# A SwiGLU down projection in sliding ranges of K, with shorter runs for its stored operands, in a hybrid transformer block

## The chip, the cores and the metric

One core of one Trainium2 chip. The metric is the device time of one execution in microseconds (us); of a kernel the median of its runs counts. Engines are named as in the profile: PE (TensorE) with PEld for its weight loads, DVE (VectorE), ACT (ScalarE), POOL (GpSimd) and SP (SyncE); here POOL and SP mostly issue DMAs, POOL on queue q0 and SP on queue q1.

## The reference

One layer of a diffusion backbone over 512 latent tokens (and 256 context tokens), width 2048. A modulation row `silu(c) @ w_mod + b_mod` gives six rows of 2048: shift, scale and gate for the mixer and for the feed-forward part. A recurrent and a windowed attention mixer feed one output projection; then comes the part that the change is about:

```python
x = x + gt_m * (concat([hg_lat, at_lat]) @ w_out)
h = modulate(rms_norm(x, norm_ffn_g), sh_f, sc_f)
gate, up = split(h @ w_gate_up)                 # 2048 -> 2 x 5632
x = x + gt_f * ((silu(gate) * up) @ w_down)     # 5632 -> 2048
```

All arrays are float32.

## The kernel before

Every product of float32 operands is made of three matmuls (`mm3`): each operand is split into a high part, rounded on ACT, and a low part, the difference formed on DVE; high x high, high x low and low x high are summed in PSUM.

The feed-forward part works on 2 x 2 blocks with a scheme of seven products (`PRODUCTS`, line 1369). So an operand is not four blocks but seven split sums of them, and a **step** (`run_step`, line 1570) is 7 products x 2 halves x 3 = 42 matmuls of 128 x 256 into seven half-used pairs of PSUM regions (`banks`). For each step SP loads two pieces of weights, 256 KB each (`st_load`, line 1393, tile `fx`, three buffers); DVE forms three sums (`st_sums`), ACT the high part `fh` (`st_high`), DVE the low part `fl` (`st_low`), each two steps ahead of the matmuls.

*Up stage*: 22 groups of 256 columns (`N_UP`), each of 8 steps over K = 2048; 176 steps. The eight operand sets of this stage are formed from x1 (`turn`, `form`). After a group's last step `evac_up` (line 1484) combines the seven results on DVE, applies the SiLU, forms the seven sums of the result, splits them (`hl`, two tiles of 128 x 1792, 896 KB each) and stores them into the DRAM buffer `sf_d` with POOL's queue: a set for the down stage.

*Down stage*: 22 such sets are the K of the product, 88 steps. Only eight sets fit into SBUF (`new_set`, line 1456, tiles `a`). K is cut into four ranges, `SPANS = (6, 6, 5, 5)` sets, and for each range the four blocks of 512 output columns (two runs of 256 in either half of the width) are visited in turn: 16 **visits** of 6 or 5 steps. At a visit's end `evac_down` (line 1539) combines the seven results with seven DVE operations into `c`, and POOL stores c in four DMAs of 256 KB to `y_d`, plainly in the first range and with an accumulating DMA in the next two. In the last range `prepare_down` (line 1519) has loaded y_d, x1 (`x1_d`, stored by POOL in `add_gated`, line 1306) and the gate row; y_d x gate + x1 is formed ahead, and c x gate is added to it and stored to the output by SP.

A set is used for the last time in a range's fourth visit. After its last step (`last_use`, line 1612) the next set takes its place, by two loads of 896 KB on POOL's queue, in runs of 7 KB. The first eight sets take the places of the up stage's during its last group.

The order of instructions on each engine is that of the code, with one exception: side work (here the modulation rows, `mod_gate` and `mod_cols`, in `mod_lane`) is woven in by a planner (`Estimate`, `Lane`), which keeps a clock for each engine and steps such a task when its operands should be there and DVE and ACT are not ahead of PE. `mod_gate` sums a row's 512 columns over K with 16 DVE operations from eight loads of 512 KB (`m_w`, SP), reduces over partitions with one matmul and stores the row in DRAM (`gtf_d`, the feed-forward gate). All tasks stand in `mod_tasks` (line 687 on) and are added before the recurrence. Since every operation passes through one wrapper, the profile gives line 130 for all; tiles tell them apart.

## Time and profile before

| what | value |
|---|---|
| median of 3 runs | 2716.01 us (2715.44 to 2721.18) |
| the profiled execution | 2721.39 us |
| its span | 2719.6 us |
| mean granted clock of PE, share of full speed | 0.97 |
| bytes moved by DMA | 488.81 MB, 180 GB/s on average |
| reloads of the sets (a from sf_d) | 44 x 896 KB, 9.8 us from issue to landing |
| loads of w_down | 176 x 256 KB, 3.7 us |
| loads of w_gate_up | 352 x 256 KB, 3.3 us |

The span lies within the profiled execution, which lasts 1.8 us longer. The up stage's matmuls run from 1239 to 2188 us, the down stage's from there to 2710 us. The granted clock has two levels, 1.2 and 2.4 GHz; 1.00 in a window means the upper one throughout. A busy time of PE counts a matmul at the lower level as long as it took there.

### The profile page before, as it was taken

To read this page: it belongs to the slowest core of one execution; us is meant where nothing else is said; L and a number is where in the kernel's file an instruction comes from. 1 tells how busy PE (TensorE), PEld (TensorE's weight loads), DVE (VectorE), ACT (ScalarE), POOL (GpSimd) and SP (SyncE) were. 2 spreads that over 40 slices of the span, in tenths; PEclk is the share of its full clock that TensorE was granted. 3 is DMA by queue.
4 is the path that set the end of the run, shared out by engine and by line. 5 is a ranking of instruction groups with operands and counts; after the bars stand their busy time and mean duration, and the time that the engine had idled before them with its cause. 6 is when DMAs were issued, how large, how long until landed. Compare 5 with 4: busy or idle time off the path is not lost.

```text
span 2719.6 us, 44137 instructions
## 1 busy us (share of the span) xinstructions
PE 2557.2 (94%) x17119; PEld 2317.3 (85%) x17119; DVE 2119.3 (78%) x3706; ACT 1060.6 (39%) x1529; POOL 219.9 (8%) x429
## 2 busy tenths in 40 slices
PE   7999999999999999997999999999999799898987
PEld 4579887878777877776999999999999789898986
DVE  4478967787899977566788888888889586766798
ACT  4244444447333332344444443434344233332322
POOL 0000010000111211100000000000000101121221
PEclk9999999999999999998999999999999899998998
DMA  9978677762654335541444444444444655677773
GB/s 347 303 262 262 214 234 224 228 193 59 203 178 126 105 120 184 174 153 55 124 156 145 147 159 144 144 163 155 136 162 153 251 202 210 197 202 197 190 205 121
DMA packets 328739, 488.81 MB, mean 180 GB/s; under 512 B 20305, under 2 KB 233458, under 8 KB 327762
## 3 DMA queue, kind: packets, MB, share of 16 engines
q1 hardware_dynamic: 284320, 354.50, 41.2%
q0 software_dynamic: 30832, 118.85, 13.5%
q10 hardware_dynamic: 13378, 12.65, 1.4%
q8 instruction: 134, 2.20, 0.3%
q14 instruction: 75, 0.61, 0.1%
HBM read 414.08 MB, written 71.84 MB: 179 GB/s over the span
## 4 chain that ended last, share of the span: by engine, by line
PE 32%; DMA 9%; DVE 8%; issue 2%; SPq 1%; ACT 0%; DVEq 0%; ACTq 0%
PE mm L130 16%; PE aux L130 16%; DMA fx<-in_w_down_dram 7%; DVE fl L130 4%; DVE big L130 3%; DVE fx L130 2%; DMA fx<-in_w_gate_up_dram 1%; SPq L130 1%; DMA gtr<-gtf_d 0%; ACT fh L130 0%; DVEq L130 0%; ACTq L130 0%
## 5 line engine op out<-in xcount | busy, mean ns | idle before, releaser
L130 ACT ACTIVATE fh<-fx 128x1792 fp32r<-128x1792 f32 x264 | 448.0, 1701 | 739.4 <-DVE fx L130 291.5
L130 DVE TENSOR_TENSOR fl<-fx,fh 128x1792 fp32r<-128x1792 f32 x264 | 532.6, 2019 | 60.6 <-ACT fh L130 58.9
L130 DVE TENSOR_TENSOR fx<-fx 128x256 f32<-128x256 f32 (+1 forms) x816 | 409.5, 510 | 213.3 <-DMA fx<-in_w_down_dram 105.9
L130 PE MATMUL mm<-a,fh 128*128 128x256 f32 x2464 | 478.6, 285 | 13.5 <-ACT a L130 12.1
L130 PE MATMUL aux<-a,fh 128*128 128x256 f32 x2464 | 475.4, 284 | 1.0 <-ACT fh L130 1.0
L130 PEld LDWEIGHTS mm<-a,fh 128*128 128x128 f32 x2464 | 388.9, 192 | 15.2 <-ACT a L130 13.0
L130 PEld LDWEIGHTS aux<-a,fh 128*128 128x128 f32 x2464 | 387.8, 191 | 1.3 <-ACT fh L130 1.2
L130 PE MATMUL aux<-a,fl 128*128 128x256 f32 x1232 | 351.6, 285 | 18.8 <-DVE fl L130 18.8
L130 PE MATMUL mm<-a,fl 128*128 128x256 f32 x1232 | 351.1, 285 | 0.0
L130 ACT ACTIVATE wh<-wr 128x512 fp32r<-128x512 f32 x376 | 227.3, 627 | 313.1 <-PE mm L130 175.9
L130 DVE TENSOR_TENSOR wl<-wr,wh 128x512 fp32r<-128x512 f32 x376 | 251.1, 685 | 89.0 <-ACT wh L130 88.3
L130 PE MATMUL mm<-wh,hT 128*128 128x512 f32 x896 | 298.6, 402 | 4.0 <-ACT hT L130 3.0
L130 PE MATMUL mm<-fh,a 128*128 128x256 f32 x1232 | 276.1, 290 | 16.5 <-DVE big L130 13.3
L130 PE MATMUL aux<-fh,a 128*128 128x256 f32 x1232 | 276.1, 290 | 7.0 <-DVE big L130 3.7
L130 PE MATMUL mm<-hT,wh 128*128 128x512 f32 x768 | 251.6, 404 | 0.0
L130 PEld LDWEIGHTS aux<-a,fl 128*128 128x128 f32 x1232 | 233.7, 190 | 19.7 <-DVE fl L130 19.7
L130 PEld LDWEIGHTS mm<-fh,a 128*128 128x128 f32 x1232 | 218.3, 198 | 19.5 <-DVE big L130 14.9
L130 PEld LDWEIGHTS mm<-a,fl 128*128 128x128 f32 x1232 | 234.1, 190 | 0.0
L130 PEld LDWEIGHTS aux<-fh,a 128*128 128x128 f32 x1232 | 217.7, 197 | 10.2 <-DVE big L130 5.2
L130 DVE SCALAR_TENSOR_TENSOR m_acc<-m_w,c_col,m_acc 128x512 f32<-128x512 f32 x240 | 178.8, 745 | 51.8 <-DMA m_w<-in_w_mod_dram 50.1
L130 PEld LDWEIGHTS mm<-wh,hT 128*128 128x128 f32 x896 | 169.4, 189 | 55.7 <-issue 8.6
L130 PE MATMUL aux<-fl,a 128*128 128x256 f32 x616 | 178.8, 290 | 23.3 <-DVE fl L130 23.3
(273 smaller groups left out, 4068.0 us busy)
## 6 DMA issues: line engine op xcount, KB each, us to landing
fx<-in_w_gate_up_dram SPq DMA_DIRECT2D x352, 256.0 KB, 3.3
wr<-in_w_in_dram SPq DMA_DIRECT2D x144, 512.0 KB, 4.6
m_w<-in_w_mod_dram SPq DMA_DIRECT2D x128, 512.0 KB, 4.7
fx<-in_w_down_dram SPq DMA_DIRECT2D x176, 256.0 KB, 3.7
sf_d<-big POOLq DMA_DIRECT2D x44, 896.0 KB, 4.1
a<-sf_d POOLq DMA_DIRECT2D x44, 896.0 KB, 9.8
ring<-in_w_mod_dram SPq DMA_DIRECT2D x64, 512.0 KB, 8.8
wr<-in_w_out_dram SPq DMA_DIRECT2D x36, 512.0 KB, 4.4
```

The lines of the kernel that those rows point to most:

```text
L130: return f(*a, **k)
```

## The change

- **Ranges that slide.** `ENDS` names for each of the 16 visits the set at which it stops; a visit starts where the visit of the same columns four earlier stopped. The visits have 2, 3, 5, 6, 6, 6, 6, 6, 6, 6, 6, 6, 8, 7, 5 and 4 steps (88 as before), and sets come free one or two to a visit, from the fourth visit on.
- **Columns.** A visit covers 512 columns that lie side by side, so a row of a w_down piece is one run of 2 KB, not two of 1 KB.
- **Stored sums.** `sf_d` is laid out so that stores and reloads have runs of 1 KB, 896 in a DMA, not 128 of 7 KB.
- **Gate and residual.** x1 is stored into `y_d` as the base. Each of the first 12 visits multiplies c by the gate (one DVE operation of 128 x 2048, a step later) and accumulates it into y_d with one DMA of 1 MB; the last four load y_d with one DMA and add. The gate's 512 columns are loaded at each visit.
- **Weight loads.** From step 8 on a step issues the load for four steps on, not three.
- **Gate row.** The four tasks for `gtf_d` join `mod_lane` at the start of the out-projection.

```diff
@@ -32,7 +32,7 @@
 RING = 5
 SC = 256
 N_UP = D_FF // SC
-SPANS = (6, 6, 5, 5)
+ENDS = (2, 3, 5, 6, 8, 9, 11, 12, 14, 15, 17, 18, 22, 22, 22, 22)
 RSQRT_SEED = float(0x5F3759DF)
 
 
@@ -194,9 +194,8 @@
     s_d = dram.tile([16, P, P], F32, name="s_d")
     gtm_d = dram.tile([1, D], F32, name="gtm_d")
     gtf_d = dram.tile([1, D], F32, name="gtf_d")
-    x1_d = dram.tile([T, D], F32, name="x1_d")
     y_d = dram.tile([T, D], F32, name="y_d")
-    sf_d = dram.tile([2 * N_UP, P, 7 * SC], F32R, name="sf_d")
+    sf_d = dram.tile([2 * N_UP, 7, P, SC], F32R, name="sf_d")
 
 
     ident = const.tile([P, P], F32, name="ident")
@@ -686,7 +685,6 @@
 
     mod_tasks = [mod_gate(j, 2 * D, gtm_d) for j in range(4)]
     mod_tasks += [mod_cols(mp, j, w) for j in range(4) for w in range(2)]
-    mod_tasks += [mod_gate(j, 5 * D, gtf_d) for j in range(4)]
 
 
 
@@ -1303,7 +1301,7 @@
             if squares:
                 act.activation(tm, x1[j][:, t, :], AF.Square, accum_out=ssj[:, t, j:j + 1])
                 if t == NT - 1:
-                    pool.dma_start(x1_d[:, 512 * j:512 * j + 512].rearrange("(t p) d -> p t d", p=P), x1[j])
+                    pool.dma_start(y_d[:, 512 * j:512 * j + 512].rearrange("(t p) d -> p t d", p=P), x1[j])
         return evac
 
     def mix_pools(st, right):
@@ -1331,6 +1329,8 @@
                 n[0] += 1
         return upto
 
+    for j in range(4):
+        mod_lane.add(mod_gate(j, 5 * D, gtf_d))
     m_st = ExitStack()
     gp = m_st.enter_context(tc.tile_pool(name="gp", bufs=1))
     mT = mix_pools(m_st, 0)
@@ -1379,16 +1379,14 @@
             u.src = [w_gate_up[(s + 8 * h) * P:(s + 8 * h + 1) * P, :].rearrange("p (u n) -> p u n", u=2)
                      [:, :, SC * g:SC * g + SC] for h in range(2)]
             steps.append(u)
-    n0 = 0
-    for b, n in enumerate(SPANS):
-        for j in range(4):
-            for s in range(n0, n0 + n):
-                u = Step()
-                u.up, u.g, u.b, u.a, u.first, u.last = False, j, b, 8 + s, s == n0, s == n0 + n - 1
-                u.src = [w_down[(2 * s + h) * P:(2 * s + h + 1) * P, :].rearrange("p (u n) -> p u n", u=2)
-                         [:, :, SC * j:SC * j + SC] for h in range(2)]
-                steps.append(u)
-        n0 += n
+    for v, e in enumerate(ENDS):
+        n0 = ENDS[v - 4] if v >= 4 else 0
+        for s in range(n0, e):
+            u = Step()
+            u.up, u.g, u.b, u.a, u.first, u.last = False, v % 4, v // 4, 8 + s, s == n0, s == e - 1
+            u.src = [w_down[(2 * s + h) * P:(2 * s + h + 1) * P, 2 * SC * (v % 4):2 * SC * (v % 4) + 2 * SC]
+                     .rearrange("p (u n) -> p u n", u=2) for h in range(2)]
+            steps.append(u)
 
     def st_load(i):
         if i < len(steps):
@@ -1507,64 +1505,51 @@
         yield
         dve.tensor_tensor(hl[1], xx[:, 1:8, :], hl[0].bitcast(F32), op=ALU.subtract)
         for i in range(2):
-            pool.dma_start(sf_d[2 * g + i].bitcast(F32), hl[i].bitcast(F32).rearrange("p f n -> p (f n)"))
-        yield
-
-    def rows_of(d, h, n, j):
-        c0 = 1024 * n + SC * j
-        return d[2 * P * h:2 * P * h + 2 * P, c0:c0 + SC].rearrange("(t p) n -> p t n", p=P)
-
-    QUADS = ((0, 1), (0, 0), (1, 1), (1, 0))
-
-    def prepare_down(j):
-
-        z = est.tile(xg, [P, 4, 512], F32, "big", "big", 4)
-        x1t = est.tile(xg, [P, 4, 512], F32, "big", "big", 4)
-        gt = est.tile(fx, [P, 2, SC], F32, "gtr", "gtr", 1)
-        for n in range(2):
-            pool.dma_start(gt[:, n, :], gtf_d[0:1, 1024 * n + SC * j:1024 * n + SC * j + SC].to_broadcast([P, SC]))
-        for k, (h, n) in enumerate(QUADS):
-            pool.dma_start(hf(z[:, k, :]), rows_of(y_d, h, n, j))
-            pool.dma_start(hf(x1t[:, k, :]), rows_of(x1_d, h, n, j))
-        yield
-        for k, (h, n) in enumerate(QUADS):
-            dve.tensor_tensor(hf(z[:, k, :]), hf(z[:, k, :]), gt[:, n:n + 1, :].to_broadcast([P, 2, SC]), op=ALU.mult)
-        yield
-        dve.tensor_tensor(z, z, x1t, op=ALU.add)
-        prepared[j] = z, gt
-        yield
+            pool.dma_start(sf_d[2 * g + i].bitcast(F32).rearrange("f p n -> p f n"), hl[i].bitcast(F32))
+        yield
+
+    def rows_of(d, j):
+        return d[:, 2 * SC * j:2 * SC * j + 2 * SC].rearrange("(a p) n -> p a n", p=P)
+
+    def quad(c, h, n):
+
+        return c[:, 2 * h:2 * h + 2, SC * n:SC * n + SC]
+
+    def prepare_down(j, fin):
+
+        gt = est.tile(fx, [P, 512], F32, "gtr", "gtr", 1)
+        pool.dma_start(gt, gtf_d[0:1, 512 * j:512 * j + 512].to_broadcast([P, 512]))
+        z = None
+        if fin:
+            z = est.tile(xg, [P, 4, 512], F32, "big", "big", 4)
+            pool.dma_start(z, rows_of(y_d, j))
+        prepared[j] = gt, z
 
     prepared = {}
 
     def evac_down(j, b, banks):
-        p1, p2, p6, p7, q4, q5, p3 = banks
-        fin = b == len(SPANS) - 1
+        p1, p2, p6, p7, q4, q5, p3 = (hf(x) for x in banks)
         c = est.tile(xg, [P, 4, 512], F32, "big", "big", 4)
-        r, t = c[:, 1, :], c[:, 3, :]
-
-        def done(k):
-            h, n = QUADS[k]
-            ck = hf(c[:, k, :])
-            if fin:
-                z, gt = prepared[j]
-                dve.tensor_tensor(ck, ck, gt[:, n:n + 1, :].to_broadcast([P, 2, SC]), op=ALU.mult)
-                dve.tensor_tensor(c[:, k, :], c[:, k, :], z[:, k, :], op=ALU.add)
-                sp_q.dma_start(rows_of(out, h, n, j), ck)
-            elif b == 0:
-                pool.dma_start(rows_of(y_d, h, n, j), ck)
-            else:
-                pool.dma_start(rows_of(y_d, h, n, j), ck, accum_op=ALU.add)
-
+        c11, r, c21, t = (quad(c, h, n) for h, n in ((0, 1), (0, 0), (1, 1), (1, 0)))
         act.activation(r, p1, AF.Copy)
-        dve.tensor_tensor(c[:, 0, :], p2, r, op=ALU.add)
+        dve.tensor_tensor(c11, p2, r, op=ALU.add)
         dve.tensor_tensor(r, p6, r, op=ALU.add)
         dve.tensor_tensor(t, r, p7, op=ALU.subtract)
-        dve.tensor_tensor(c[:, 2, :], t, q4, op=ALU.add)
+        dve.tensor_tensor(c21, t, q4, op=ALU.add)
         dve.tensor_tensor(r, q5, r, op=ALU.subtract)
         dve.tensor_tensor(t, q5, t, op=ALU.subtract)
         dve.tensor_tensor(r, p3, r, op=ALU.add)
-        for k in (0, 2, 3, 1):
-            done(k)
+        gt, z = prepared[j]
+        if z is None:
+            yield
+            dve.tensor_tensor(c, c, gt[:, None, :].to_broadcast([P, 4, 512]), op=ALU.mult)
+            pool.dma_start(rows_of(y_d, j), c, accum_op=ALU.add)
+        else:
+            for h, n in ((0, 1), (1, 1), (1, 0), (0, 0)):
+                ck = quad(c, h, n)
+                dve.tensor_tensor(ck, ck, gt[:, None, SC * n:SC * n + SC].to_broadcast([P, 2, SC]), op=ALU.mult)
+                dve.tensor_tensor(ck, ck, quad(z, h, n), op=ALU.add)
+                sp_q.dma_start(quad(rows_of(out, j), h, n), ck)
         yield
 
     def run_step(i, hooks):
@@ -1587,11 +1572,14 @@
     turn(0, 0)
     turn(0, 1)
     form(0)
-    pending = list(range(8, 8 + sum(SPANS)))
+    pending = list(range(8, 8 + N_UP))
     last_use = {u.a: i for i, u in enumerate(steps)}
     tail = []
     for i, u in enumerate(steps):
-        st_load(i + 3)
+        if i <= 8:
+            st_load(i + 3)
+        if i >= 8:
+            st_load(i + 4)
         st_sums(i + 2)
         st_high(i + 2)
         hooks = {}
@@ -1600,11 +1588,11 @@
         run_step(i, hooks)
         form(i + 1)
         st_low(i + 2)
-        if not u.up and u.b == len(SPANS) - 1 and u.first:
-            tail.append(prepare_down(u.g))
         for g in list(tail):
             if next(g, tail) is tail:
                 tail.remove(g)
+        if not u.up and u.first:
+            prepare_down(u.g, u.b == len(ENDS) // 4 - 1)
         if u.last:
             g = evac_up(u.g, u.banks) if u.up else evac_down(u.g, u.b, u.banks)
             next(g)
@@ -1613,7 +1601,7 @@
             n = pending.pop(0)
             new_set(n)
             for k in range(2):
-                pool.dma_start(sets[n][k].bitcast(F32).rearrange("p f n -> p (f n)"), sf_d[2 * (n - 8) + k].bitcast(F32))
+                pool.dma_start(sets[n][k].bitcast(F32), sf_d[2 * (n - 8) + k].bitcast(F32).rearrange("f p n -> p f n"))
 
 
 _INS = ["x", "c", "ctx", "c_ctx", "w_mod", "b_mod", "norm_mix_g", "norm_ffn_g", "w_in", "hg_lb",
```

What this does to the order on the queues is seen at two places. On POOL, the kernel before at the end of the down stage's first range (a: sets, reloaded from sf_d):

```order
L130 DMA y_d<-big 128x2x256 x12
L130 DMA a_22726<-sf_d 128x1792
L130 DMA a_22727<-sf_d 128x1792
L130 DMA a_22782<-sf_d 128x1792
L130 DMA a_22783<-sf_d 128x1792
L130 DMA a_22838<-sf_d 128x1792
L130 DMA a_22839<-sf_d 128x1792
L130 DMA a_22894<-sf_d 128x1792
L130 DMA a_22895<-sf_d 128x1792
L130 DMA a_22950<-sf_d 128x1792
L130 DMA a_22951<-sf_d 128x1792
L130 DMA y_d<-big 128x2x256 x4
```

and the changed kernel from the start of its down stage:

```order
L130 DMA y_d<-big 128x4x512
L130 DMA gtr<-gtf_d 128x512
L130 DMA y_d<-big 128x4x512
L130 DMA gtr<-gtf_d 128x512
L130 DMA a_22314<-sf_d 128x7x256
L130 DMA a_22315<-sf_d 128x7x256
L130 DMA y_d<-big 128x4x512
L130 DMA gtr<-gtf_d 128x512
L130 DMA a_22370<-sf_d 128x7x256
L130 DMA a_22371<-sf_d 128x7x256
L130 DMA a_22654<-sf_d 128x7x256
L130 DMA a_22655<-sf_d 128x7x256
```

Twelve y_d stores and then five sets in a row have become one accumulation, the gate's load and one or two sets a visit.

On SP, in the out-projection (wr: weights of that projection; io: its other operand; gt_c: the mixer's gate; fx: first weights of the up stage), the kernel before:

```order
L130 DMA gt_c<-gtm_d 128x512
L130 DMA wr<-in_w_out_dram 128x2x512 x6
L130 DMA io<-mix_d 128x512 x3
L130 DMA wr<-in_w_out_dram 128x2x512
L130 DMA io<-mix_d 128x512 x3
L130 DMA wr<-in_w_out_dram 128x2x512
L130 DMA io<-mix_d 128x512 x2
L130 DMA wr<-in_w_out_dram 128x2x512
L130 DMA fx<-in_w_gate_up_dram 128x2x256 x3
L130 DMA wr<-in_w_out_dram 128x2x512
L130 DMA fx<-in_w_gate_up_dram 128x2x256 x3
L130 DMA wr<-in_w_out_dram 128x2x512 x3
```

and the changed kernel:

```order
L130 DMA gt_c<-gtm_d 128x512
L130 DMA wr<-in_w_out_dram 128x2x512 x3
L130 DMA m_w<-in_w_mod_dram 128x2x512 x3
L130 DMA wr<-in_w_out_dram 128x2x512
L130 DMA m_w<-in_w_mod_dram 128x2x512
L130 DMA wr<-in_w_out_dram 128x2x512
L130 DMA m_w<-in_w_mod_dram 128x2x512 x2
L130 DMA wr<-in_w_out_dram 128x2x512
L130 DMA m_w<-in_w_mod_dram 128x2x512 x2
L130 DMA wr<-in_w_out_dram 128x2x512 x3
L130 DMA fx<-in_w_gate_up_dram 128x2x256
L130 DMA io<-mix_d 128x512 x2
```

Loads of w_mod for the feed-forward gate (m_w), 22 in all, now stand between the weights; before, all of them came earlier. Among the weights of the feed-forward part SP's order is the same in both kernels, but for one or two loads that change places with output stores at the end.

## Rows read from the trace of the kernel before

**Rows 1.** The page's head: the span, and busy time (share) xinstructions by engine.

```profile
span 2719.6 us, 44137 instructions
PE 2557.2 (94%) x17119; PEld 2317.3 (85%) x17119; DVE 2119.3 (78%) x3706; ACT 1060.6 (39%) x1529; POOL 219.9 (8%) x429
```

**Rows 2.** Windows: stretch, length, busy (x) by engine, PEclk, DMA share, GB/s.

```profile
1400.00:1800.00 400.00, 400.00 (x3334) 399.91 (x3333) 353.35 (x446) 166.93 (x119) 10.68 (x20) 1.00 0.46 151
2100.00:2719.60 619.60, 540.51 (x4227) 530.87 (x4225) 454.98 (x584) 182.61 (x123) 102.22 (x134) 0.93 0.64 198
2200.00:2300.00 100.00, 99.27 (x828) 98.36 (x828) 80.94 (x103) 35.32 (x23) 11.84 (x18) 1.00 0.51 172
```

**Rows 3.** Timeline at the end: start us, us, engine, line, operation.

```profile
2710.09 0.28 PE L130 MATMUL aux<-fh,a 128*128 128x256 f32 x1
...
2710.71 1.28 DVE L130 TENSOR_TENSOR big<-mm,big 128x512 f32<-128x512 f32 x2
2711.91 0.68 DVE L130 TENSOR_TENSOR big<-aux,big 128x512 f32<-128x512 f32 x1
```

**Rows 4.** The chain that ended last, down stage: start us, us, what.

```profile
2158.12 20.03 DMA fx<-in_w_down_dram
...
2429.95 21.00 DMA fx<-in_w_down_dram
```

**Rows 5.** Waits from 2120 to 2720 us: total us, times, longest us.

```profile
DVE fx L130 <- DMA fx<-in_w_down_dram: 105.9, 32, 11.2
...
PE aux L130 <- DVE fl L130: 42.1, 10, 9.6
...
DVE fx L130 <- DMA fx<-in_w_gate_up_dram: 25.3, 3, 12.8
...
PE mm L130 <- DVE big L130: 13.3, 11, 3.0
...
PE aux L130 <- DVE big L130: 3.7, 7, 2.1
```

**Rows 6.** DMA queues from 2162 to 2176 us: packets, MB, share of 16 engines.

```profile
q0 software_dynamic: 771, 4.90, 84.9%
q1 hardware_dynamic: 823, 0.79, 17.2%
```

**Rows 7.** DMA queues from 2256 to 2263 us, where one visit's y_d is stored.

```profile
q0 software_dynamic: 320, 1.05, 41.3%
```

**Rows 8.** DMA queues from 1188 to 1200 us, SP loading in 2 KB runs.

```profile
q1 hardware_dynamic: 701, 1.37, 36.3%
```

**Rows 9.** DVE by shape, 2120 to 2720 us: busy us, mean ns | idle.

```profile
L130 DVE TENSOR_TENSOR fl<-fx,fh 128x1792 fp32r<-128x1792 f32 x95 | 191.2, 2018 | 14.7 <-ACT fh L130 14.6
L130 DVE TENSOR_TENSOR fx<-fx 128x256 f32<-128x256 f32 x186 | 77.6, 421 | 3.7
L130 DVE TENSOR_TENSOR fx<-fx 128x512 f32<-128x512 f32 x93 | 63.6, 687 | 131.2 <-DMA fx<-in_w_down_dram 105.9 <-DMA fx<-in_w_gate_up_dram 25.3
...
L130 DVE TENSOR_TENSOR big<-big 128x2048 f32<-128x2048 f32 x4 | 9.1, 2282 | 0.0
```

**Rows 10.** Timeline at a gate row's matmul; in brackets the idle time before it.

```profile
720.64 2.04 PE L130 MATMUL aux<-m_acc,ones 128*128 128x512 f32 x2 [6.27 <-DVE hP L130]
```

**Rows 11.** Windows behind that matmul and in the out-projection, columns as in rows 2.

```profile
720.00:740.00 20.00, 19.36 (x73) 15.13 (x74) 17.64 (x58) 6.66 (x10) 2.54 (x8) 0.87 0.67 200
1000.00:1200.00 200.00, 192.55 (x883) 157.35 (x882) 122.69 (x210) 69.86 (x141) 15.88 (x38) 0.99 0.55 178
```

**Rows 12.** Waits of the whole span, the sums of the modulation rows.

```profile
DVE m_acc L130 <- DMA m_w<-in_w_mod_dram: 50.1, 45, 3.0
```

**Rows 13.** POOL's groups, columns as in rows 9.

```profile
L130 POOL DMA_DIRECT2D y_d<-big x48 | 50.9, 1158 | 271.7 <-DVE big L130 271.4 <-issue 0.3
```

**Rows 14.** DMA queues from 2530 to 2540 us, accumulating into y_d.

```profile
q0 software_dynamic: 797, 0.77, 57.4%
```

## The prediction, made before the changed kernel ran

> **What bounds the kernel now.** I read the page first: TensorE (PE) is busy 94% of the 2719.6 us [rows 1], so time can only go where PE idles or runs at the lower clock. The windows then show where that is. In the middle of the up stage 3334 matmuls fill 400.00 us at clock 1.00: 0.120 us for one, so 42 x 0.12 = 5.04 us for a step. From 2100 us to the end 4227 matmuls run at a mean clock of 0.93 [rows 2]. At 0.120 us they would need 507 us. The last matmul starts at 2710.09 and takes 0.28 [rows 3], which leaves 9.2 us of evacuation and stores behind it. So 619.6 - 507 - 9.2 = **103 us** are lost in the down stage and the last two up groups: 70 as idle time (619.6 - 540.5 busy - 9.2) and 33 as matmuls at the lower of the two clock levels (540.5 - 507), which follow the idle times. The stage is not slow as such: from 2200 to 2300 us PE is busy 99.27 of 100 [rows 2].
>
> The chain that ended last says what ends the idle time: single weight loads of 256 KB with pieces of 20 and 21 us [rows 4]. The waits agree: VectorE (DVE), which makes the sums of the weights, waits 105.9 us for w_down and 25.3 for w_gate_up, and PE behind it 42.1 us for the low parts [rows 5]. The DMA view of such a stretch says why. For 14 us queue 0 (POOL: reloads of the sets) and queue 1 (SP: weights) share the 16 engines, whose shares sum to 102%: 771 packets with 4.90 MB against 823 with 0.79 MB [rows 6]. They take turns about one for one, but a packet of POOL holds 6.4 KB on average and takes 0.849 x 16 x 14 / 771 = 0.247 us (7 KB: 0.28), one of SP 1 KB and 0.047 us. So the weights get 0.79 MB / 14 us = 56 GB/s, and a step needs 512 KB in 5.04 us = 104 GB/s. Ten or so such loads of 896 KB stand in one burst behind the last quarter of a range.
>
> **The change, part by part.**
>
> *Ranges that slide.* The bytes stay: 14 of the 22 sets are reloaded during the down stage, each 1.84 MB. But one or two sets come free in a visit instead of up to six in every fourth. The first of these loads is issued ten steps into the stage, and no set is used before 16 steps (81 us) have passed after its load: two sets take 3.7 MB / 300 GB/s = 12 us. Their place behind a visit's accumulation on POOL's queue, which waits for a multiplication one step later, costs 5 us of these 81, so nothing.
>
> *Runs of 1 KB for the sets, 2 KB for w_down.* What a turn takes now comes from two rows. In the stores of y_d, also runs of 1 KB, 1.05 MB took 0.413 x 16 x 7 = 46 us of engine time, 0.044 us for each KB, in 320 packets, few enough for four runs or 4 KB in one (1.05 MB is 256 times 4 KB) [rows 7]: 0.18 us. A 2 KB run of SP took 0.363 x 16 x 12 / 701 = 0.10 us [rows 8]. A pair of turns is 0.28 us, and the weights get 16 x 2 KB / 0.28 us = 115 GB/s, above the 104 they need. So I take the whole **-103**. Bounds: -103 (nothing is left to win) and -52, where half has a cause that I don't see.
>
> *The first burst stays.* While the last up group runs, eight sets and two stores, 18 MB, are moved, and w_gate_up keeps its 1 KB runs: 16 x 1 KB / (0.05 + 0.18) = 71 GB/s for some three steps of loads. Two steps of weights lie ready. Between 0 and the 25.3 us of now [rows 5], nearer to the low end: **+4**.
>
> *Short visits first.* A visit's end costs DVE seven operations of 0.68 [rows 3] and now a multiplication of 2.28 [rows 9]: 7.1 us. A step costs 0.687 + 2 x 0.421 + 2.018 = 3.55 [rows 9]. Visits 0 to 3 have 16 steps: 16 x 3.55 + 4 x 7.1 + 9.7 for the last up group (the same seven, two products, sums, low part) = 95 us of DVE against 80.6 of PE. Operations overlap by 0.08 us (0.68 long, 0.60 apart [rows 3]), 109 of them by 9: 86. Up to 5.6 us behind, or 0 if DVE starts ahead: **+4**. The whole stage fits: 88 x 3.55 + 16 x 4.8 + 12 x 2.28 + 32 x 0.68 + 9.7 = 447, with the overlap of 521 operations 405, against 443.5 for PE.
>
> *Ends of visits.* PE waits 13.3 + 3.7 = 17.0 us for banks that DVE still reads [rows 5]. There are 16 visits as before, and some of these waits only stand behind late weights. Between 0 and 17: **+8.5**.
>
> *Gate row later.* Its sums leave the recurrence, where PE waited 6.27 us before the row's matmul [rows 10] and ran the next 20 us at 0.87 (2.6 us) [rows 11]: up to -8.9. Three gates' sums, 48 operations of 0.75 us, and 22 loads of 512 KB enter the out-projection. There DVE has 122.7 of 200 us [rows 11], so 36 more fit, and 178 GB/s become 236, a share of 0.73 for 0.55. The loads stand on SP between those of w_out; late, they hold up DVE by up to 3.0 us each, 1.1 on average [rows 12], which its slack covers. The last gate's matmul and store now stand just ahead of the sum of squares at the stage's end: between 0 and those 8.9, taken at 2.5. Sum **-6.4**.
>
> *The rest is nothing.* One accumulation of 1 MB for four of 256 KB, x1 as the base in y_d: 4 MB less to read, and DVE's 12 x 2.28 in place of 16 x 0.68 + 4 x 2.28, covered as above. POOL issues a store of 256 runs in 1158 ns [rows 13]; 896 runs at four times that, 88 times, are 408 us of an engine that is 8% busy [rows 1], with 16 steps of cover; with that cover gone a set would come 4 us later. The load "a step sooner" moves no weight load past another on SP: each still waits for the low parts of the step whose buffer it takes, and only the output stores change places with one or two loads. The 9.2 us behind the last matmul keep their operations.
>
> Sum: -103 + 4 + 4 + 8.5 - 6.4 = -92.9. 2719.6 - 92.9 = 2626.7 of span; the profiled execution took 2721.4, 1.8 more, so 2628.5; it lay 5.4 above the median of 2716.01, so **2623**.
>
> **The rivals.**
>
> *A turn of POOL stays long* (0.13). If one turn takes as many 1 KB runs as it likes, say the 7 KB of a partition, it lasts 0.28 us as now [rows 6], a pair 0.38, and the weights get 86 GB/s; with 17 KB 0.68 + 0.10, and 42. A visit's one or two sets last 6 to 12 us, in which 17 to 60% of the need is missing: 1 to 7 us a burst, against two steps of weights in hand. 25.7 MB in all would lose 15 to 43 us; a third of the upper end reaches PE, +14: 2637, at most 2666. Against it speak the packets of the y_d stores, which end at four runs [rows 7].
> The Trainium skill ("DMA: Bandwidth & Descriptors", section "Queues, rings and completion order") says that an engine drains a whole packet, typically some 9 to 17 descriptors, from one ring before it turns to the next. By that rule the 1 KB runs would not shorten POOL's turns at all. The trace shows one 7 KB run to a turn [rows 6] and four 1 KB runs [rows 7], fewer than the page's typical packet; no run here yet shows this form of load.
>
> *DVE becomes the bound* (0.12): with no overlap its 447 us pass PE's 443.5 by 3.5, and the ends of visits keep all of their 17.0: +12, 2635. For it: it is busy 80.9 of 100 us even where nothing starves [rows 2]; against it: that leaves 19.
>
> *Half the loss stays* (0.08): the wait for weights has a second cause, such as 256 KB loads landing late whenever anything else moves: 2623 + 52 = 2675. For it: some pieces of the chain lie between bursts.
>
> *The DMA engines become the bound, and it is slower* (0.05). Place: the sets' 1 KB runs on POOL's queue. If each is a packet of its own at the price of an accumulated KB, 0.574 x 16 x 10 / 797 = 0.115 us, 0.122 for a whole KB [rows 14], then sets and accumulations, 2464 + 768 + 512 KB for each engine with gates and finals, take 457 us, and the weights 146 (2816 KB at 0.10 for 2 KB [rows 8]): 603 us from the first reload at about 2128 on (at full rate the down steps begin at 2100 + (4227 - 88 x 42) x 0.12 = 2164, the reloads seven steps ahead). End 2731, with the tail 2740, on the median's scale 2736. It decides at (478.7 + 93 - 146) / 3744 KB = 0.114 us for a KB, where 478.7 = 35.2 + 88 x 5.04 is the time from that reload to PE's own end. Plain stores take 0.044 [rows 7], so 0.05.
>
> *The change doesn't do what it says* (0.02): a reload is still late or the weights still starve at each visit, and what the bursts cost is only spread out: about 2716.
>
> **How the numbers follow.** My forecast has 0.60. All residual terms at zero and the gate row at its best give 2623 - 16.5 - 2.5 = 2604, so the range begins at 2603; its top is the first rival's 2666. That leaves out half the loss staying, the slower case and the void one: 0.15. A measurement of this kernel can tell about 0.2% from no change. Faster by more: 0.60 + 0.13 + 0.12 + 0.08 = 0.93; within it 0.02; slower 0.05.
>
> **What would show it.** Right: in the down stage the granted clock is 1.00 in nearly every window, DVE's wait for w_down falls from 105.9 to under 15 us, q0 packets of the sets hold about 4 KB, the chain has no weight piece over 10 us, and the row's 6.27 us wait is gone. Wrong: weight waits of over 30 us (first or third rival; packet size tells which), PE waits for DVE of over 25 us while no weight is late (second), a DMA share near 1.0 through the stage (slower case), or new PE idle time in the out-projection beside m_w loads.

## The result, and the profile after

The changed kernel takes 2743.43 us (median of 4 runs, 2739.19 to 2745.73) beside 2715.73 us of the kernel before on the same chip: ratio 1.0096, 95% interval 1.0077 to 1.0115, so **26 us slower** where 93 us less were forecast. The time lies near the slower rival's 2736, but its mechanism is not what happened.

Windows of the changed kernel, columns as in [rows 2]:

```profile
1400.00:1800.00 400.00, 398.12 (x3300) 396.54 (x3301) 348.52 (x440) 166.34 (x119) 19.56 (x20) 1.00 0.49 149
2180.00:2730.00 550.00, 481.86 (x3720) 470.49 (x3719) 407.31 (x508) 157.69 (x107) 59.10 (x64) 0.93 0.64 185
```

and the tile view of fh in the kernel before and in the changed one (duration min/median/max, first and last start of the up stage's matmuls), then the last matmul of the changed kernel in the timeline:

```profile
L130 PE MATMUL mm<-a,fh x2464: 274/282/582, 1239.0 to 2187.3; 128*128 128x256 f32 x190
```

```profile
L130 PE MATMUL mm<-a,fh x2464: 274/282/580, 1237.8 to 2182.1; 128*128 128x256 f32 x190
```

```profile
2730.35 0.28 PE L130 MATMUL aux<-fh,a 128*128 128x256 f32 x1
```

So the up stage ends 5 us earlier, and the down stage lasts 548 us (2182 to 2730.6) where it lasted 522 (2188 to 2710.4 [rows 3]). PE needs 443.5. The mean clock is 0.93 as before, and the DMA engines are busy 0.64 of the stage, also as before: over the stage they are not full (beside a set's loads they are for some 10 us at a time, as a window further down shows). The waits from 2100 to 2741 us say where the time goes (total us, times, longest):

```profile
DVE fx L130 <- DMA fx<-in_w_down_dram: 132.4, 44, 8.6
...
DVE fx L130 <- DMA fx<-in_w_gate_up_dram: 21.6, 6, 9.7
...
PE aux L130 <- DVE fl L130: 30.2, 8, 6.7
...
PE mm L130 <- DVE big L130: 16.9, 10, 4.5
...
PE aux L130 <- DVE big L130: 9.8, 14, 3.0
```

DVE's wait for w_down, 105.9 us in 32 pieces [rows 5], is 132.4 in 44. The 20 us pieces are gone from the chain; in most visits there are now one or two of 8 to 11:

```profile
2223.07 8.45 DMA fx<-in_w_down_dram
...
2256.83 8.97 DMA fx<-in_w_down_dram
...
2271.77 9.60 DMA fx<-in_w_down_dram
...
2302.42 9.31 DMA fx<-in_w_down_dram
...
2337.61 10.21 DMA fx<-in_w_down_dram
```

The place of the last of these, DVE, then ACT, POOL and PE in the timeline (start us, us, what, in brackets the idle time before):

```profile
2331.06 2.01 DVE L130 TENSOR_TENSOR fl<-fx,fh 128x1792 fp32r<-128x1792 f32 x1
2332.99 2.28 DVE L130 TENSOR_TENSOR big<-big,gtr 128x2048 f32<-128x2048 f32 x1
2335.19 2.02 DVE L130 TENSOR_TENSOR fl<-fx,fh 128x1792 fp32r<-128x1792 f32 x1
2337.13 0.69 DVE L130 TENSOR_TENSOR fx<-fx 128x512 f32<-128x512 f32 x1
2343.11 2.03 DVE L130 TENSOR_TENSOR fx<-fx 128x512 f32<-128x512 f32 x5 [5.29 <-DMA fx<-in_w_down_dram]
2347.92 0.69 DVE L130 TENSOR_TENSOR fx<-fx 128x512 f32<-128x512 f32 x1 [2.78 <-DMA fx<-in_w_down_dram]
2348.53 2.02 DVE L130 TENSOR_TENSOR fl<-fx,fh 128x1792 fp32r<-128x1792 f32 x1
...
2344.97 3.29 ACT L130 ACTIVATE fh<-fx 128x1792 fp32r<-128x1792 f32 x2 [11.54 <-DVE fx L130]
...
2331.82 1.94 POOL L130 DMA_DIRECT2D a<-sf_d  x2 [29.44 <-PE aux L130]
2335.59 1.33 POOL L130 DMA_DIRECT2D y_d<-big  x1 [1.84 <-DVE big L130]
...
2350.60 0.58 PE L130 MATMUL aux<-fl,a 128*128 128x256 f32 x1 [3.50 <-DVE fl L130]
```

A visit's multiplication releases its accumulation at 2335.6, beside a set's loads. A low part that ends frees a weight buffer, and only then is the next load issued: here one behind the low part that ends at 2333.1, one behind that of 2337.2. DVE has 4.8 and 2.6 us of other work, then it stands 5.3 us before the sum that needs the first of these loads and 2.8 us before the sum that needs the second. **The low parts of two earlier steps stand behind this last sum** in DVE's order, though ACT had made the high part of the one by 2346.7 (that of the other by 2348.3), and PE, out of low parts, stands 3.5 us. In the stretch 2180 to 2730 DVE's work and its wait for w_down are 407.3 + 131.3 = 539 of 550 us: DVE has no time left in which to catch up.

The order on DVE is not that of the code, as the section on the kernel before has it: in the code a step's low part comes before the next step's sums, while the trace has the first sum of a step ahead of the low part of the step before it in 56 of the 88 down steps, and ahead of two low parts in 13 (76 and 5 in the kernel before). The scheduler behind the code makes this order; f1 below changes it.

### The profile page after: what moved, and what is told of

Its sections match the earlier page's. It is cut to its first block, busy times and chain, and to the rows that moved or that the text cites. A ratio compares the mean times of both kernels' runs of the same rounds, so it can differ in the third digit from the quotient of the medians.

```text
span 2740.1 us, 44026 instructions
## 1 busy us (share of the span) xinstructions
PE 2561.0 (93%) x17119; PEld 2318.1 (85%) x17119; DVE 2130.8 (78%) x3698; ACT 1060.0 (39%) x1529; POOL 207.0 (8%) x373
## 4 chain that ended last, share of the span: by engine, by line
PE 22%; DVE 13%; DMA 12%; issue 4%; ACT 1%; SPq 1%; DVEq 0%; ACTq 0%
PE mm L130 11%; PE aux L130 10%; DMA fx<-in_w_down_dram 8%; DVE fl L130 6%; DVE big L130 5%; DMA fx<-in_w_gate_up_dram 4%; DVE fx L130 2%; ACT fh L130 1%; SPq L130 1%; DVEq L130 0%; ACTq L130 0%; ACT big L130 0%
## 5 line engine op out<-in xcount | busy, mean ns | idle before, releaser
L130 DVE TENSOR_TENSOR fx<-fx 128x256 f32<-128x256 f32 (+1 forms) x816 | 405.3, 510 | 250.9 <-DMA fx<-in_w_down_dram 132.4
L130 PE MATMUL mm<-fh,a 128*128 128x256 f32 x1232 | 278.2, 292 | 18.8 <-DVE big L130 16.9
## 6 DMA issues: line engine op xcount, KB each, us to landing
a<-sf_d POOLq DMA_DIRECT2D x44, 896.0 KB, 11.8
```

The lines of the kernel that those rows point to most:

```text
L130: return f(*a, **k)
```

## The experiments

All ratios are to the kernel before on the same chip, with 95% intervals. The kernel before differs by up to 8 us between chips, so versions are compared by their ratios: 0.001 is 2.7 us, and the changed kernel stands at 1.0096.

| run | ratio | interval | us against the changed kernel |
|---|---|---|---|
| e4 no multiplications | 1.0055 | 1.0040 to 1.0070 | -11 |
| e5 no reloads | 0.9974 | 0.9960 to 0.9987 | -33 |
| e6 no accumulations | 0.9954 | 0.9941 to 0.9967 | -39 |
| e7 two queues | 1.0999 | 1.0981 to 1.1017 | +245 |
| f1 low part first | 0.9994 | 0.9978 to 1.0010 | -28 |
| e8 sets on SP | 0.9968 | 0.9952 to 0.9984 | -35 |
| f6 four weight buffers | 0.9581 | 0.9558 to 0.9603 | -140 |
| f7 the same, sets on SP | 0.9553 | 0.9534 to 0.9572 | -147 |
| e1 runs of 7 KB | 1.0005 | 0.9987 to 1.0023 | -25 |
| e2 four ranges | 1.0130 | 1.0088 to 1.0172 | +9 |
| e3 gate row early | 1.0049 | 1.0030 to 1.0068 | -13 |
| h1 before, four weight buffers | 0.9711 | 0.9675 to 0.9747 | -105 |
| i1 low part first, 7 KB | 0.9958 | 0.9943 to 0.9972 | -37 |
| i2 multiplication later | 1.0084 | 1.0064 to 1.0104 | -3 |
| i3 four buffers, 7 KB, gate row early | 0.9542 | 0.9521 to 0.9563 | -150 |
| i4 the same, sets on SP | 0.9563 | 0.9543 to 0.9584 | -145 |
| j1 before, runs of 1 KB | 1.0030 | 1.0010 to 1.0051 | -18 |
| j2 as i3, four ranges | 0.9527 | 0.9506 to 0.9548 | -155 |

**What is taken away.** Three runs leave one kind of work out of the changed kernel.

```diff
-            dve.tensor_tensor(c, c, gt[:, None, :].to_broadcast([P, 4, 512]), op=ALU.mult)      # e4
+            if not u.up:                                                                        # e5
+                sets[n] = sets[u.a]
+                continue
-            pool.dma_start(rows_of(y_d, j), c, accum_op=ALU.add)                                # e6
```

> The changed kernel without its 12 multiplications of c by the gate (the gate is left out of all visits but the last four). Late weights (my theory): in the changed kernel DVE is busy or waiting for weights all through the down stage, about 415 us of work and 132 us of waits in 548, and a pair of steps' weights takes 9 to 10 us while POOL's transfers run, 3.8 otherwise. Then 12 x 2.28 = 27 us less work shortens what stands between two waits, but the weights come when they come: 10 to 27 us faster than the changed kernel's 2743, with the wait for w_down growing. DVE's work alone (rival): the full 27 us or more, with no more waiting than before. DMA engines full (rival): no change.

> The changed kernel without the 14 reloads of sets in the down stage (28 transfers of 896 KB; a set that comes free is used again as it stands, so the later ranges have wrong operands); the eight sets of the first burst are still loaded. Late weights: the waits for w_down fall from 132 to 50 us or less, what is left being the first burst and the accumulations; 60 to 90 us faster than 2743. DMA engines full: 25.7 MB of some 130 MB in the stage, a fifth of 548 us, so 100 us or more. DVE's work alone: no change.

> The changed kernel without the 12 accumulations of 1 MB into y_d (the output then holds only the last four visits and x1). Late weights: an accumulation holds the engines for some 6 us beside a set's 8, and both hit the same two pairs of steps of a visit, so 20 to 40 us faster than 2743. DMA engines full: 12 of some 130 MB, at twice the price, 60 to 80 us. DVE's work alone: no change.

They gave 11, 33 and 39 us. The first says that DVE's work alone is not the bound: 27 us of it went, 11 came out, and the wait for w_down rose to 137.1 us. It does not price the multiplications alone: without them DVE's order changes too (a first sum stands ahead of two low parts in 2 steps, not 13), and the accumulations are issued 0.4 us after a visit's last sum, not some 4.5, beside the next sets' loads; weight loads there took up to 14 us, 11 in the changed kernel. The second missed its 60 to 90 us; the third came out at the top of its 20 to 40. Neither POOL transfer alone is the whole cost, and far less came than the bytes would be worth if the engines were full throughout. What is left is enough to make a load late: without any reload, DVE still waits:

```profile
DVE fx L130 <- DMA fx<-in_w_down_dram: 102.8, 32, 8.4
```

**More turns for the weights.** The second load of each step on ACT's queue.

```diff
-                sp_q.dma_start(u.x[:, 2 * h:2 * h + 2, :], u.src[h])
+                (sp_q, act)[h].dma_start(u.x[:, 2 * h:2 * h + 2, :], u.src[h])
```

> The changed kernel with the second of each step's two weight loads issued by ACT on its own queue. Late weights, by turns between queues: in a round an engine then moves two weight packets of 2 KB for one of POOL's 4 KB, so a pair of steps takes 16 x (0.10 + 0.10 + 0.19) = 6.3 us and not 32 x 0.29 = 9.3; the waits for w_down fall by half or more, 40 to 80 us faster than 2743. If the waits come from full engines, or from DVE's own work, the time stays within 10 us of 2743.

A miss by 300 us, which tells nothing of the turns: ACT now waits, in its own order, for the low part that frees the buffer, and the high parts stand behind it. The waits of the whole span:

```profile
ACT fh L130 <- DVE fx L130: 702.6, 137, 12.0
DVE fx L130 <- DMA fx<-in_w_gate_up_dram: 323.5, 148, 5.3
...
ACT fh L130 <- DVE fl L130: 189.3, 42, 8.7
```

The last of these lines stands nowhere in the changed kernel's waits. The up stage, with no set to load until its end, slows down too (1140 us from first to last start, 944 in the changed kernel), while the loads of w_gate_up land almost as before (3.2 us on SP, 3.9 on ACT, 3.3 in the changed kernel): the loop from low part to load to sum is what it hits.

**The loop itself.** The loop is this: a step's low part frees a buffer, the freed buffer lets SP issue a load, and DVE needs that load for a later step's sum. f1 fixes DVE's order; e8 takes the sets off POOL; f6 gives the loads a fourth buffer; f7 is f6 with e8.

```diff
+            with tc.issue_after(steps[i - 2].low.ins) if i >= 2 else ExitStack():               # f1
                 dve.tensor_tensor(xx[:, 4:6, :], xx[:, 0:1, :].to_broadcast([P, 2, SC]), xx[:, 1:3, :], op=ALU.add)
...
```

```diff
+        for _ in range(4 if i < 182 else 2):                                                    # e8
+            if pieces and pieces[0][0] <= i:
+                sp_q.dma_start(*pieces.pop(0)[1:])
...
-                pool.dma_start(sets[n][k].bitcast(F32), sf_d[2 * (n - 8) + k].bitcast(F32).rearrange("f p n -> p f n"))
+                for f in range(0, 7, 2):
+                    pieces.append((i + 3, sets[n][k].bitcast(F32)[:, f:min(f + 2, 7), :],
+                                   sf_d[2 * (n - 8) + k].bitcast(F32).rearrange("f p n -> p f n")[:, f:min(f + 2, 7), :]))
```

```diff
-            u.x = est.tile(fx, [P, 8, SC], F32, "fx", "fx", 3)                                  # f6
+            u.x = est.tile(fx, [P, 4, SC], F32, "fx", "fx", 4)
...
+            ss = steps[i].s = est.tile(fx, [P, 4, SC], F32, "fs", "fs", 2)
...
-            act.activation(u.hi, u.x[:, 1:8, :], AF.Copy)
+            act.activation(u.hi[:, 0:3, :], u.x[:, 1:4, :], AF.Copy)
+            act.activation(u.hi[:, 3:7, :], u.s, AF.Copy)
```

(and the low part, the sums of the up stage's sets and their split in the same way)

> The changed kernel with one order fixed on DVE: the first sum of a step is issued behind the low part of the step two before it. In the changed kernel the scheduler puts that sum, which waits for weights, ahead of two finished steps' low parts after each multiplication (12 times); in the kernel before it stands ahead of one. Theory now: three weight buffers mean that a load is issued only when the low part three steps earlier is done, and DVE has only 3 to 4 us of other work before it needs that load, so what a load takes over 3 to 4 us is lost on DVE, and DVE with 26 of 30 us a visit cannot make it up. Then the 2.0 us of one low part move from behind the wait to ahead of it, 12 times: 15 to 30 us faster than 2743. If the place of the wait doesn't matter because DVE is ahead anyway: within 5 us of 2743.

> The changed kernel with all 22 sets reloaded by SP in pieces of 256 KB, two a step (four during the first burst), behind a step's weight loads and three steps after the set came free, and not by POOL. Weights and sets then stand in one queue and take no turns; a weight load has at most two pieces ahead of it, 1.6 us at 0.05 us for a packet of 1 KB. Taking the reloads away in the down stage gave 28 us. If it was the turns with POOL's long bursts that cost this: 15 to 40 us faster than 2743, the first burst included. If any bytes ahead of the weights cost the same: within 10 us of 2743, or slower.

> The changed kernel with the weight tile parted: four buffers for the 4 KB that are loaded and two for the sums (24 KB as before), high and low parts in two instructions each, so that a load is issued when the low part four steps earlier is done. Theory of the short loop: DVE then has 7 us of other work between issuing a load and needing it, not 3.5; the two or three late loads of each visit lose 3.5 us less each, so the waits for w_down fall from 132 to 60 us or less, and the time by 50 to 90 us, to 2655 to 2695. Rivals: if the engines are full, the weights come no sooner and the time stays within 10 us of 2743; if DVE's work is the bound, the extra instructions (264 of some 0.1 us) make it slower.

> Four buffers for the loaded weights and the sets reloaded by SP in pieces, together. Theory of the short loop: what the two give adds up as far as there are waits left: 70 to 110 us faster than 2743, 2633 to 2673, below the kernel before. If each alone did nothing, neither will both.

f1 gave 28 us and e8 35, within what was expected. f6 gave 140, more than the 50 to 90 expected, and f7 147 for 70 to 110. The waits of f6 from 2100 us on, and its windows:

```profile
DVE fs L130 <- DMA fx<-in_w_down_dram: 11.3, 14, 2.8
...
PE mm L130 <- DVE fl L130: 9.4, 1, 9.4
```

```profile
2145.00:2590.00 445.00, 434.16 (x3629) 432.36 (x3627) 401.03 (x572) 165.32 (x188) 57.90 (x63) 0.99 0.76 230
```

The same bytes go through in less time (DMA share 0.76, not 0.64), the median landing of a w_down load is even longer (7.8 us, 4.2 in the changed kernel), and PE's clock is 0.99: a late load costs next to nothing here once it is issued early enough. Part of the 140 lies outside the down stage, some of it where the up stage's first weights arrive: from 1240 to 1400 us, f6 first and then the changed kernel,

```profile
1240.00:1400.00 160.00, 158.62 (x1315) 157.51 (x1316) 151.57 (x227) 87.60 (x100) 6.47 (x7) 1.00 0.44 136
```

```profile
1240.00:1400.00 160.00, 146.39 (x1140) 142.51 (x1139) 123.91 (x156) 70.36 (x55) 4.51 (x5) 0.95 0.35 108
```

That is 175 matmuls more, 21 us. Over the whole up stage (first and last start, f6),

```profile
L130 PE MATMUL mm<-a,fh x2464: 274/281/387, 1240.5 to 2140.8; 128*128 128x256 f32 x190
```

f6 takes 900 us where the changed kernel takes 944. So 44 us were won there, and the down stage lasts 454 us, not 548: 94 us, a little over what was expected of it. Not all of this need be the buffer: f6 changes DVE's order too (no first sum stands ahead of two low parts any more), for which f1 alone gave 28 us. f7 is not surely better than f6; the intervals meet.

**Parts undone, alone.**

```diff
-    sf_d = dram.tile([2 * N_UP, 7, P, SC], F32R, name="sf_d")                                   # e1
+    sf_d = dram.tile([2 * N_UP, P, 7 * SC], F32R, name="sf_d")
-ENDS = (2, 3, 5, 6, 8, 9, 11, 12, 14, 15, 17, 18, 22, 22, 22, 22)                               # e2
+ENDS = (6,) * 4 + (12,) * 4 + (17,) * 4 + (22,) * 4
+    mod_tasks += [mod_gate(j, 5 * D, gtf_d) for j in range(4)]                                  # e3
-    for j in range(4):
-        mod_lane.add(mod_gate(j, 5 * D, gtf_d))
```

> The changed kernel with the stored sums back in runs of 7 KB. By turns, a pair of steps' weights then takes 32 x (0.10 + 0.28) = 12.2 us beside a set's load and not 9.3; 14 sets of 8 us (then 6) in the down stage meet one to two pairs each, and DVE loses 2.9 us at each: 25 to 60 us slower than 2743. If the length of runs doesn't matter (as many packets of SP get through for each byte of POOL): within 10 us.

> The changed kernel with the four fixed ranges of before (6, 6, 5, 5 sets), all else as changed. What my prediction held, that the bursts are what costs: 50 us or more slower than 2743. Theory of the short loop: the same bytes hold up the weights for the same time, in bursts or spread, and bursts even leave visits undisturbed in which DVE keeps its place: within 15 us of 2743.

> The changed kernel with the four tasks of the feed-forward gate back among the early ones. My prediction gave the later place 6.4 us. The up stage began 1.2 us earlier than before (1237.8 against 1239.0), so what was won in the recurrence was lost in the out-projection: within 5 us of 2743.

> The kernel before with nothing but the parted weight tile: four buffers for the 4 KB that are loaded, two for the sums. Theory of the short loop: it holds for the kernel before too, whose down stage and last up groups lose 103 us; single loads in its bursts take 20 us, of which 7 and not 3.5 are then covered, and the short waits go: 40 to 80 us faster than 2716, so 2636 to 2676, slower than the 2608 of the changed kernel with the same edit, whose pairs take 9. If the changed kernel's other parts give nothing even then, this one is at 2608 too or below.

e1 went the other way: **the runs of 7 KB are 25 us faster**. The profile page's line on the reloads (KB each, median us to landing) shows where to look, changed kernel first, then e1:

```profile
a<-sf_d POOLq DMA_DIRECT2D x44, 896.0 KB, 11.8
```

```profile
a<-sf_d POOLq DMA_DIRECT2D x44, 896.0 KB, 8.3
```

With short runs a set's load lasts longer. That a load of weights which meets it is late until it has passed is a reading, not shown by itself; it agrees with DVE's wait for w_down, 115.7 us in e1. The weights' better share of the turns bought nothing. In the up stage too, the stores in 1 KB runs cost some matmuls (3300 from 1400 to 1800 us); e1 has there

```profile
1400.00:1800.00 400.00, 399.87 (x3333) 399.69 (x3332) 353.60 (x445) 167.17 (x119) 10.63 (x20) 1.00 0.46 151
```

e2 bears out the second theory: the four ranges are 9 us slower, with intervals that meet. The bursts were not what made the loss; the sliding moved the same bytes to other times. e3 missed by a little: the early place is 13 us faster (intervals just apart). It begins the up stage no sooner (1238.1 us), so the gain is not where the gate's sums were or are; it shows only further down (of 9 us between the two profiled spans 6 lie in the up stage and 3 in the down stage, with a wait for w_down of 125.8 us). Why stays open.

h1: the kernel before gains 79 us by the parted tile alone, within what was expected. Its up stage,

```profile
L130 PE MATMUL mm<-a,fh x2464: 277/282/582, 1233.2 to 2133.7; 128*128 128x256 f32 x190
```

takes 900 us for 948, which is 48 of them; 25 lie in the down stage (498 us for 522). It remains 35 us slower than f6: with the loop loosened, something in the change is a gain. What, j2 narrows down below.

**Together, and the place of an accumulation.**

```diff
-            yield                                                                               # i2
-            dve.tensor_tensor(c, c, gt[:, None, :].to_broadcast([P, 4, 512]), op=ALU.mult)
+            yield
+            yield
+            with tc.issue_after(steps[i + 4].low.ins):
+                dve.tensor_tensor(c, c, gt[:, None, :].to_broadcast([P, 4, 512]), op=ALU.mult)
```

i1 is f1 with e1; i3 is f6 with e1 and e3; i4 is i3 with the sets on SP as in e8; j1 puts nothing but the runs of 1 KB into the kernel before; j2 is i3 with e2.

> The changed kernel with the order on DVE fixed (a step's first sum behind the low part two steps before) and the runs of 7 KB back. Alone the two gave 22 and 19 us. If they are separate costs (the place of the wait, and how long a set holds the engines): 35 to 41 us faster than 2743, 2702 to 2708, below the kernel before, so that the rest of the change is a gain of some 10 us. If both shorten the same wait: 20 to 25 us.

> The changed kernel with each of the 12 multiplications, and so its accumulation of 1 MB, issued behind the low part one step later. Leaving the accumulations out gave 36 us, leaving the multiplications out 6, so it is the transfer that costs, and in the changed kernel it is issued 2 us ahead of the load that DVE needs next. If the place costs: 10 to 25 us faster than 2743. If an accumulation costs the same wherever it stands: within 8 us.

> The changed kernel with four buffers for the loaded weights (2608), runs of 7 KB for the sets and the gate row among the early tasks. The last two gave 19 and 7 us alone. With the waits for w_down at 11 us, only the first burst is left for the runs: 0 to 8 us for them, and 3 to 7 for the gate row: 2595 to 2605. If the parts add up: 2582.

> The same with the sets reloaded by SP in pieces of two blocks. It gave 7 us with the runs of 1 KB; what it takes from is the first burst: 2588 to 2600, the fastest so far; 2595 to 2605 if the longer runs have won the same already.

> The kernel before with nothing but the stored sums in runs of 1 KB (sets and stores in turns of 4 KB, weights in 1 KB still). Ten loads of a burst are 560 KB for each engine: now 80 turns of 7 KB, 80 x 0.33 = 26 us in which the weights get 80 KB, 2.4 steps of the 5.2 that PE wants; then 140 turns of 4 KB, 140 x 0.24 = 34 us with 4.4 of 6.7 steps. What my prediction held (the weights' share is what counts): half a step, 2.5 us, less lost in a burst, 10 us faster than 2716 in all. Theory that a late load is late until the burst has passed (as the longer runs in the changed kernel showed): each burst lasts 8 us longer, 5 to 25 us slower than 2716.

> The fastest version so far (four buffers for the loaded weights, runs of 7 KB, gate row early; 2595) with the four fixed ranges of before. It tells what the sliding ranges are worth where a load may be late by 7 us: bursts of ten loads last 26 us, so 3 bursts lose some 10 us each: 20 to 40 us slower than 2595. If the buffer alone takes up the bursts too: within 8 us of 2595.

i1 came out as expected, 37 us below the changed kernel and 11 below the kernel before: order on DVE and length of runs together turn a small gain into the loss. They are not separate costs altogether: alone, by ratios, they gave 28 + 25 = 53. i2 moved nothing that can be told; since DVE's order changed with it, it says only that this later place is no cure. i3 takes 2595 us (0.9542), below both kernels; with the waits gone, runs and gate row together give 4 thousandths beside f6, with intervals that meet, and i4 shows nothing more for the sets on SP. The interval of i3 meets those of f6, i4 and j2. j1: short runs cost the kernel before 8 us (3 to 14), at the low end of what the second theory said. j2 at 0.9527 shows that with four buffers **the sliding ranges are worth nothing that can be measured** either way: the buffer takes up the bursts too. In j2's down stage nothing is left to win, PE is busy nearly throughout at the upper clock:

```profile
2145.00:2590.00 445.00, 440.40 (x3687) 437.29 (x3685) 409.30 (x587) 166.58 (x190) 43.47 (x62) 1.00 0.73 229
```

j2 also tells which parts of the change pay. It has neither the sliding ranges nor the short runs nor the late gate row; next to h1 it has only the columns side by side with their 2 KB runs, the new way of gate and residual, and the load a step sooner. Yet it is 0.0184, some 50 us, faster than h1. No run parts these three. The waits from 2100 us on name two places, DVE's wait for weights and PE's for banks; h1 first, then j2:

```profile
DVE fs L130 <- DMA fx<-in_w_down_dram: 60.5, 14, 7.3
...
PE mm L130 <- DVE big L130: 26.1, 7, 9.3
...
PE aux L130 <- DVE big L130: 7.3, 6, 3.4
```

```profile
DVE fs L130 <- DMA fx<-in_w_down_dram: 17.3, 14, 3.1
...
PE mm L130 <- DVE big L130: 2.0, 4, 1.0
...
PE aux L130 <- DVE big L130: 1.9, 4, 1.0
```

## Why the prediction was wrong

- **The step that failed** is the one that took the whole -103 because the weights would get 115 GB/s, "above the 104 they need". Of the -103 nothing came: the down stage lasts 26 us longer. Yet the turns were about as forecast. From 2160 to 2176 us of the changed kernel, where sets and stores move in runs of 1 KB and nothing is accumulated, and from 2338 to 2350 us, with an accumulation, the queues show

```profile
q0 software_dynamic: 1170, 4.47, 80.4%
```

```profile
q0 software_dynamic: 923, 2.54, 83.7%
q1 hardware_dynamic: 441, 0.79, 21.7%
```

  that is 3.8 KB and 0.18 us for a packet of POOL at first, 2.8 KB and 0.17 us then, and 0.095 us for one of SP. (The first rival, with turns of 7 KB and more, is out.) The two shares of the second window sum to 105%: the engines are full there. The loads of two steps, 32 packets for each engine, then take 32 x 0.27 = 8.6 us, an estimate from these rows, and the chain has 8.5 to 10.2. But a rate is not a time of arrival. Before, 64 turns of 1 KB and 7 KB took 64 x 0.33 = 21 us, the chain's 20 and 21 [rows 4]; the edit halved a late load, and made of 32 waits of up to 11.2 us 44 of up to 8.6. What the runs showed in its place is the loop that lets a load start: with it loosened the down stage takes 454 us (f6) in place of 548.
- **"Two steps of weights in hand"** was never so; the prediction used it for the first burst and for the first rival. A buffer is free after a step's low part, and DVE then has 3 to 4 us of other work, that of one step, before the sum that needs the next load (4.8 and 2.6 in the stretch above). A load of w_down landed in 3.7 us at the median before; what it takes beyond that, DVE waits. The working looked at SP's order (the same in both kernels, which held) but not at DVE's, where the multiplication made the scheduler put a sum ahead of two low parts; f1 prices that at 28 us.
- **DVE's slack** was worked out right, 405 us of work for 443.5, and 407 were measured in the stretch. But it was set against DVE's work alone, and the weights' waits were taken as gone. A visit of six steps has 30.2 us for PE and, with 6 x 3.55 + 4.8 + 2.28 less the overlap of 32 operations, 26 for DVE: 4 us to make up waits, of which there were some 9 (132.4 us over 88 / 6 visits).
- **Ends of visits**: PE's waits for banks rose from 17.0 to 16.9 + 9.8 = 26.7 us, not to 8.5. They go with late weights, as the prediction half said: in f6, where hardly a wait for weights is left, they are 0.5; in h1, with 60.5 us of such waits, 33.4.
- **The burst and the sets**: no engine waited for a set, as forecast. The first burst's wait for w_gate_up is 21.6 us for 25.3, not 4, again for lack of weights in hand.
- **The gate row** was given -6.4. The up stage began 1.2 us earlier, and e3 says that the late place costs 13. In the out-projection PE lost what it had won:

```profile
1000.00:1200.00 200.00, 183.94 (x826) 149.28 (x827) 139.06 (x232) 64.78 (x134) 21.23 (x45) 0.96 0.63 205
```

  826 matmuls at 0.96 for 883 at 0.99 [rows 11]; 36 us of sums were said to fit beside the 122.7, and the cover did not hold.
- **The slower rival** gave 2736 with the DMA engines full. The time is near by chance: a packet of the sets cost 0.04 to 0.06 us for a KB, not 0.12, and the engines were busy 0.64. The rival nearest to what happened had the smallest chance, 0.02: "the weights still starve at each visit, and what the bursts cost is only spread out". It put that at 2716; what it lacked is the new order on DVE and the longer landing of short runs, for which together i1 gives 37 us. The sign to look for was named ("weight waits of over 30 us"), but given to other rivals.

## What to carry to other kernels

Ask of a prefetched load not only whether its queue has the rate, but what releases its issue and what stands on the consumer between that release and the use: here three buffers looked like two steps ahead and were one. Where a small engine works 26 of every 30 us, as here, its waits become the kernel's time, and shortening the bursts only traded few long waits for many short ones; one more buffer, bought by parting a tile into what is loaded and what is computed, was worth 79 us before the change and 140 after it, 48 and 44 of them in a stage that the change hardly touches. Price a change of many parts part by part: of the two in the title the sliding ranges gained nothing that can be measured and the short runs lost 25 us; with four buffers some 50 us of gain lie in the other parts. Look at the order on the engine that waits, not only on the queues, when operations are added under a scheduler.

## What was not expected of the hardware

- Runs of 1 KB instead of 7 KB made the same 896 KB land in 11.8 us (median) instead of 8.3 beside weight loads, and 13.2 instead of 9.8 in the kernel before (j1), and cost 25 and 8 us of the whole. With four buffers (f6 and i3) the longer landing, 15.5 us for 12.6, costs nothing that can be measured.
- The second queue for weights cost 245 us, by what stood behind the issuing instruction on ACT (189.3 us of waits that the changed kernel does not have), while the transfers landed almost as before (3.9 and 3.2 us for 3.3).
